# Last down product of the second block: low parts of the weights on VectorE, its and TensorE's order pinned unit by unit, normalised rows in tiles of their own

## The chip, the cores and the metric

The kernel runs on one core of one Trainium2 chip. Its time is the device time of one execution in microseconds; for the kernel before, three executions took 2285.23, 2288.1 and 2289.94 us, so the median is 2288.1 us. Lower is better.

## What is computed

A trunk of two layers over 1024 rows of 1024 numbers in float32. Each layer has a token mixer (latent attention in the first, differential attention in the second) and a SwiGLU block, both with a residual and a layer norm:

```python
def _swiglu(x, w_gu, w_down):
    gate, up = jnp.split(x @ w_gu, 2, axis=-1)
    return (jax.nn.silu(gate) * up) @ w_down
...
    h = _layernorm(ALPHA * h + _swiglu(h, ffn_w_gu[i], ffn_w_down[i]), ln_ffn_g[i], ln_ffn_b[i])
```

The change concerns the very last part of this: the end of `@ w_down` of the second layer, and the layer norm of the rows that it completes, which are stored as the output.

## The kernel before, in words

**Products in three passes.** TensorE multiplies fp32r operands. A float32 operand is split into a high part (a cast on ScalarE, L503) and a low part (the difference, L504, on VectorE or GpSimd); a product of two such pairs is high x high, high x low and low x high, three matmuls (`step`, L815 on).

**The down product in seven.** The down product of a block is cut into halves in each of its three dimensions and done as seven products of half-size blocks (Strassen's scheme), so the operands of most of them are sums or differences of blocks. The hidden values come from a DRAM scratch `h_dr`, already combined; the blocks of the weights are combined on the fly. Each product has 11 units (11 slices of 128 along the hidden dimension). A unit needs one tile of hidden values `op_h` (made by `from_h`) and one tile of weights, and gives three matmuls for each of four accumulators, one PSUM bank for each 128 rows (`t` or `tb`, 0 to 3).

**The last product**, named "4", adds to the four banks `dw_0` to `dw_3`, which hold the result of the product before it. For each unit j, the work ahead of the matmuls is

- on VectorE, `rw_t` minus `tt` (L805): the weights of this product are the difference of a block that is loaded in three groups (`rw_t`, in `w_block`) and a block kept from before (`tt`);
- on ScalarE two casts (L503), to the high parts `wt` and `op_h`;
- the two low parts (L504): that of the hidden values on VectorE, that of the weights on GpSimd (`split(..., G)`).

In the last block (`next_x is None`) the loop over the units issues only the banks 0 and 1; then `last(0)` and `last(1)` close them, and the banks 2 and 3 follow, each with all 11 units. `last(t)` adds the bank to its residual row block `z` (L834, the sum comes out too) and normalises it. `layer_norm` (L163 on) gives the means on VectorE (L166, L167), two sums of squares on ScalarE (L170), `y = (z - mean) * g` on VectorE (L176), the variance (L178), its power on GpSimd (L180), and `y * rs + b` on VectorE (L183), which is stored by SyncE's DMA queue. Here y is z itself: the row block is overwritten in place.

**What sets the order.** Every engine executes its own list in order. A scheduler makes the lists by priority and by its own estimate of when things are ready; `behind(i, j)` (L155 on) holds instruction i after instruction j in a list without a wait. Before the change the low parts of `op_h` and the subtractions L805 are held only behind the reads of the banks (`banks_read[-1]`). Loads are issued by SyncE's queue in the order in which `load_down` was called.

Of the kernel before, what the change touches and what calls it, by code (L numbers as in the profile page):

```python
# [9 lines left out]
F32 = mybir.dt.float32  # L10
F32R = mybir.dt.float32r
AF = mybir.ActivationFunctionType
ALU = mybir.AluOpType
# [29 lines left out]
def trunk(  # L43
# [33 lines left out]
    V, A, G, T = nc.vector, nc.scalar, nc.gpsimd, nc.tensor  # L77
# [29 lines left out]
    def f32(t):  # L107
        return t.bitcast(F32)

    def big_tile(name, dt=F32R):  # L110
        return big.tile([P, 2, 1024], dt, tag="big", name=name)
# [43 lines left out]
    def behind(i, j):  # L155

        tc.add_manual_dep(
            i, j.name,
            mybir.DependencyInfo(mybir.DependencyClass.NoSync, mybir.DependencyReason.DATA),
            reason="kept in program order",  # L160
        )
# [186 lines left out]
    class OutProj:  # L348
# [54 lines left out]
        def split(self, tb, hs, o):  # L403
            oh, ol = (t[:, hs] for t in self.oh[tb])
            A.activation(oh, o, AF.Copy, scale=self.scale)
            V.scalar_tensor_tensor(ol, o, self.scale, f32(oh), ALU.mult, ALU.subtract)
# [99 lines left out]
    turns = {"op": 0}  # L506

    def op_unit(src, eng, name, tags=("wh", "wl"), pool=None):

        tag = tags[turns["op"] % len(tags)]  # L510
        turns["op"] += 1
        where = wp if tag in ("wh", "wl") else pool
        t = where.tile([P, 2, 512], F32R, tag=tag, name=f"op_{name}", bufs=6 if pool is where else 3)
        turns["last"] = split((t[:, 0], t[:, 1]), src, eng)
        return t

    def swap(side):
        return "left" if side == "right" else "right"

    def ffn(side, xo, xst, pending, layer, x_src, x_dst, lng, lnb, next_x, spare=()):  # L520
# [4 lines left out]
        nm = f"f{layer}"  # L525
# [10 lines left out]
        r, tmp, ops, acc, hp, pg = {}, {}, {}, {}, {}, {}  # L536
# [192 lines left out]
        for i in (1, 0):  # L729
# [7 lines left out]
        lo_half, hi_half = slice(0, 512), slice(512, 1024)  # L737
# [3 lines left out]
        tt = {  # L741
            j: poolx.tile([P, 2, 512], F32, tag=f"tt{j}", name=f"tt{layer}_{j}")
            for j in (range(11) if swap(side) == "left" else reversed(range(11)))
        }

        chain, in_order, banks_read = [], [], []

        def load_down(dst, src):

            i = nc.sync.dma_start(dst, src).ins  # L750
            if in_order:
                behind(i, chain[-1])
            chain.append(i)

        def from_h(s, name, tags=tags, late=False):

            for gi, (j0, j1) in enumerate(groups):
                r = poolh.tile([P, 4, 512], F32, tag="rawh", name=f"rh{layer}_{name}_{gi}")
                load_down(r[:, :j1 - j0], h_dr[gi][s, :, :j1 - j0, :])
                for j in range(j0, j1):  # L760
                    t = op_unit(r[:, j - j0], V, f"h{layer}_{name}_{j}", tags, pool)
                    if late and j > 1:
                        behind(turns["last"], banks_read[-1])
                    yield t

        def w_block(kh, cs, name):

            for gi, (j0, j1) in enumerate(groups):
                r = big_tile(f"rw{layer}_{name}_{gi}", F32).rearrange("p a (b c) -> p (a b) c", b=2)
                src = w_dn[layer, 11 * kh + j0:11 * kh + j1, :, cs].rearrange("f p c -> p f c")  # L770
                load_down(r[:, :j1 - j0], src)
                for j in range(j0, j1):
                    yield r[:, j - j0]

        def unit(src, name, eng=G, tags=tags):
            return op_unit(src, eng, f"w{layer}_{name}", tags, pool)


        def b11():
            for j in range(11):  # L780
                load_down(tt[j], w_dn[layer, j].rearrange("p (b c) -> p b c", b=2))
                yield unit(tt[j][:, 0], f"b11_{j}", V if j < early else G)
# [18 lines left out]
                yield unit(r, f"{name}_{j}")  # L801

        def t4():
            for j, r in enumerate(w_block(1, lo_half, "t4")):
                i = V.tensor_tensor(r, r, tt[j][:, 0], ALU.subtract).ins  # L805
                if j > 1:
                    behind(i, banks_read[-1])
                if next_x is not None:
                    yield unit(r, f"t4_{j}", G, ("o",))
                    continue  # L810
                t = poolx.tile([P, 2, 512], F32R, tag=f"tt{j}", name=f"wt4{layer}_{j}")
                split((t[:, 0], t[:, 1]), r, G)
                yield t

        def step(o, h, w, tb, first, last):  # L815
            c = slice(tb * P, (tb + 1) * P)
            for a, b_ in ((0, 0), (0, 1), (1, 0)):
                T.matmul(  # L818
                    o, h[:, a, c], w[:, b_], start=(first and (a, b_) == (0, 0)), stop=(last and a == 1),
                    skip_group_check=True,  # L820
                )

        def whole(o, hs, ws, first):
            for j, (h, w) in enumerate(zip(hs, ws)):
# [7 lines left out]
        def added(half, cs, o, tb, acc=None, scale=1.0):  # L832
            n = rows(half, tb)
            banks_read.append(V.scalar_tensor_tensor(  # L834
                z[n][:, cs], z[n][:, cs], scale, o, ALU.mult, ALU.add,
                **({} if acc is None else {"accum_out": sums[n][:, acc:acc + 1]}),
            ).ins)

        def finish(tb, junk, y=None):
            y = z[tb] if y is None else y  # L840
            return layer_norm(z[tb], sums[tb], junk, y, g, b, f"{nm}_{tb}", x_dst[tb * P:(tb + 1) * P, :],
                              2 if next_x is None and tb == 3 else 1)

        def accumulators(name, tag):
            if tag == "x":
                return [ps_s(f"d{name}{layer}_{t}") for t in range(4)]
            return [(ps_m if t < 2 else ps_t)(f"d{name}{layer}_{t}") for t in range(4)]
# [5 lines left out]
        hs, ws = from_h(0, "1"), b11()  # L853
        with tc.high_priority(100):
            hs, ws = (itertools.chain([next(x) for _ in range(early)], x) for x in (hs, ws))
        x4, y4 = accumulators("x", "x"), accumulators("y", "y")
# [6 lines left out]
        hs = from_h(3, "5")  # L863
        hs = itertools.chain([next(hs)], hs)
# [17 lines left out]
        y4 = accumulators("w", "y")  # L882
# [11 lines left out]
        for t in range(4):  # L894
            added(1, hi_half, y4[t], t, 1)

        def last(t):
            added(1, lo_half, y4[t], t, 0)
            finish(t, [y4[t], y4[t]])

        new, rest, normed = None, [], []
        if next_x is None:
            hs, ws = [], []
            for h, w in zip(from_h(2, "4", late=True), t4()):
                hs.append(h)
                ws.append(w)
                for t in range(2):
                    step(y4[t], h, w, t, False, len(hs) == 11)
            stx.close()
            last(0)  # L910
            last(1)
            for t in range(2, 4):
                for j in range(11):
                    step(y4[t], hs[j], ws[j], t, False, j == 10)
                last(t)
        else:
            gb = big_tile(f"gb_{nm}", F32)
            for i, src in enumerate((lng, lnb)):
                nc.gpsimd.dma_start(gb[:, i], src.partition_broadcast(P))
            whole(y4, from_h(2, "4", ("o",)), t4(), False)  # L920
            stx.close()
            new = next_x()
            with tc.high_priority(60):
                for t in range(4, 8):
                    to_xT(z[t], new, t, f"{nm}_{t}", (ps_s, ps_s))

            yb = [big_tile(f"y_{nm}_{i}", F32) for i in range(2)]
            junk = wp.tile([P, 2, 512], F32, tag="wr", name=f"junk_{nm}", bufs=2)
            for t in range(4):
                y = yb[t // 2][:, t % 2]  # L930
                V.scalar_tensor_tensor(
                    y[:, lo_half], z[t][:, lo_half], 1.0, y4[t], ALU.mult, ALU.add, accum_out=sums[t][:, 0:1]
                )
                A.copy(y[:, hi_half], z[t][:, hi_half])
            for t in range(4):
                y = yb[t // 2][:, t % 2]
                normed.append(layer_norm(
                    y, sums[t], [junk[:, 0], junk[:, 1]], y, gb[:, 0], gb[:, 1], f"{nm}_{t}",
                    x_dst[t * P:(t + 1) * P, :],
                ))  # L940
                rest.append(lambda t=t, y=y: to_xT(y, new, t, f"{nm}_{t}", (ps_t, ps_s)))
# [24 lines left out]
    with tc.tile_pool(name="a0", bufs=2, side="right") as pool:  # L966
# [92 lines left out]
        done = []  # L1059
        for tbs in ((0, 1), (2,), (3,), (4,), (5,), (6,), (7,)):  # L1060
# [6 lines left out]
            done = [(tb, latents(tb, *m)) for tb, m in zip(tbs, ms)]  # L1067
# [179 lines left out]
    with ExitStack() as st:  # L1247
# [11 lines left out]
        for ql in q_lo:  # L1259
            for mp in range(2):  # L1260
                b = slice(64 - mp * 64, 128 - mp * 64)
                z = bb[b, :512]
                i = G.tensor_tensor(ql[b, mp * 512:mp * 512 + 512], z, z, ALU.subtract).ins
# [260 lines left out]
```

## Time and profile before

| what | value |
|---|---|
| median of three executions | 2288.1 us (2285.23 to 2289.94) |
| the profiled execution's own time | 2289.88 us |
| its span, first to last instruction | 2288.1 us |
| TensorE busy, share of the span | 2245.8 us, 98% |
| VectorE, ScalarE, GpSimd busy | 1556.8, 1015.4, 864.0 us |
| granted TensorE clock, mean | 0.997 |

All times in the profile are microseconds from the start of the span, so the profiled execution spends 1.78 us outside of it. The last product's matmuls stand from 2242.45 on. A row of the timeline gives start, duration, engine, line, operation, output and inputs, and in brackets how long the engine was idle ahead of it and what ended that. Consecutive instructions of an engine overlap by a little: the step from one start to the next is what each costs in a row.

### The profile page before, as it was taken

Reading aid. Unit: us, or ns where it says so; the run is one execution under the profiler, and the core shown is the slowest. Engines: PE = TensorE matmul, PEld = TensorE weight load, DVE = VectorE, ACT = ScalarE, POOL = GpSimd, SP = SyncE. Lnnn points to the kernel's source line nnn. Section 1 sums busy time; section 2 is a strip of 40 time slices with the busy share of each in tenths; the row PEclk is TensorE's granted clock in tenths of the full one; section 3 lists DMA queues with packets and bytes.
Section 4 is the critical chain, followed back from the end, with each engine's and each line's share of the span. In section 5 each row is a group of like instructions: output and inputs, shape, how many; then the busy total and the mean of one; then the engine's idle time right before and its main releaser. Section 6 shows DMA issues by size and latency. Waiting matters only on the chain.

```text
span 2288.1 us, 31118 instructions
## 1 busy us (share of the span) xinstructions
PE 2245.8 (98%) x11410; PEld 1913.3 (84%) x11410; DVE 1556.8 (68%) x2837; ACT 1015.4 (44%) x2097; POOL 864.0 (38%) x687
## 2 busy tenths in 40 slices
PE   8999999999999999999999999999999999999997
PEld 8999998878888887888889898988778888877886
DVE  5676665686666658677576666676776665668777
ACT  4455564342333324344465655564432333234353
POOL 2232341114444435555432423221024444436563
PEclk9999999999999999999999999999999999999998
DMA  5010125334444428444311212154254131338353
GB/s 201 14 35 31 41 72 198 140 132 151 151 152 179 151 103 331 184 179 149 106 45 31 70 28 66 33 200 155 92 175 143 69 138 69 138 115 317 132 205 119
DMA packets 105544, 288.28 MB, mean 126 GB/s; under 512 B 7968, under 2 KB 30112, under 8 KB 94896
## 3 DMA queue, kind: packets, MB, share of 16 engines
q1 hardware_dynamic: 100976, 275.87, 33.9%
q0 software_dynamic: 4416, 10.42, 1.6%
q8 instruction: 90, 1.47, 0.3%
q14 instruction: 62, 0.51, 0.1%
HBM read 205.00 MB, written 77.07 MB: 123 GB/s over the span
## 4 chain that ended last, share of the span: by engine, by line
PE 90%; DVE 4%; DMA 3%; issue 1%; ACT 1%; POOL 1%; SPq 0%; DVEq 0%; POOLq 0%; ACTq 0%
PE gb L549 14%; PE gc L549 10%; PE ga L549 10%; PE dw L818 7%; PE s_a L219 4%; PE zp_a L417 3%; PE dx L818 3%; PE s_b L219 3%; PE dv L818 3%; PE dy L818 3%; PE bp L145 3%; PE bp L143 3%; PE bp L144 3%; PE o_a L262 2%; PE o_b L262 2%; PE hq L1023 1%
## 5 line engine op out<-in xcount | busy, mean ns | idle before, releaser
L503 ACT CAST op_g<-gr 128x512 fp32r<-128x512 f32 x240 | 146.8, 621 | 370.1 <-PE gb L549 182.3
L504 POOL TENSOR_TENSOR op_g<-gr,op_g 128x512 fp32r<-128x512 f32 x104 | 146.6, 1415 | 247.9 <-ACT op_g L503 139.9
L504 DVE TENSOR_TENSOR op_h<-rh,op_h 128x512 fp32r<-128x512 f32 x154 | 162.5, 1083 | 63.7 <-ACT op_h L503 63.6
L549 PE MATMUL ga<-xh_m,op_g 128*128 128x512 f32 x512 | 168.2, 389 | 0.0
L503 ACT CAST op_h<-rh 128x512 fp32r<-128x512 f32 x154 | 92.9, 620 | 139.7 <-PE dx L818 38.0
L818 PE MATMUL dw<-op_w_t,op_h 128*128 128x512 f32 x660 | 151.3, 390 | 0.0
L818 PEld LDWEIGHTS dw<-op_w_t,op_h 128*128 128x128 f32 x660 | 123.5, 188 | 26.0 <-DVE op_h L504 0.4
L227 ACT ACTIVATE l_b<-l_b,mx_b 128x256 f32<-128x256 f32 (+7 forms) x128 | 99.4, 777 | 76.4 <-DVE mx_b L222 72.4
L818 PE MATMUL dx<-op_w_b,op_h 128*128 128x512 f32 x528 | 122.5, 391 | 7.4 <-ACT op_w_b L503 3.9
L1328 POOL TENSOR_SCALAR l_b<-l_b,rb,cst 128x128 f32<-128x128 f32 (+3 forms) x64 | 52.5, 820 | 204.4 <-DVE rb L1327 193.0
L504 POOL TENSOR_TENSOR op_w_t<-tt,op_w_t 128x512 fp32r<-128x512 f32 x66 | 98.7, 1499 | 80.7 <-ACT op_w_t L503 80.1
L818 PEld LDWEIGHTS dx<-op_w_b,op_h 128*128 128x128 f32 x528 | 98.5, 188 | 31.0 <-ACT op_w_b L503 4.7
L504 DVE TENSOR_TENSOR op_g<-gr,op_g 128x512 fp32r<-128x512 f32 x136 | 110.6, 819 | 14.5 <-ACT op_g L503 14.3
L549 PE MATMUL gb<-t4h_f,op_g 128*128 128x512 f32 x352 | 115.9, 390 | 3.7 <-DVE tmp L632 3.7
L504 POOL TENSOR_TENSOR op_g<-s,op_g 128x512 fp32r<-128x512 f32 x40 | 54.8, 1369 | 170.1 <-ACT op_g L503 161.9
L549 PE MATMUL gb<-t2h_f,op_g 128*128 128x512 f32 x352 | 115.6, 390 | 0.4 <-DVE op_g L504 0.4
L549 PE MATMUL gc<-t1h_f,op_g 128*128 128x512 f32 x352 | 115.6, 389 | 0.1
L549 PE MATMUL gc<-b22h_f,op_g 128*128 128x512 f32 x352 | 115.3, 389 | 0.0
L549 PE MATMUL gb<-t3h_f,op_g 128*128 128x512 f32 x352 | 115.2, 389 | 0.0
L549 PEld LDWEIGHTS ga<-xh_m,op_g 128*128 128x128 f32 x512 | 96.1, 188 | 20.0
L143 PE MATMUL bp<-xT_f,h_wb 128*128 128x512 f32 x256 | 101.7, 397 | 0.0
L144 PE MATMUL bp<-xT_f,h_wb 128*128 128x512 f32 x256 | 101.5, 397 | 0.0
(382 smaller groups left out, 6736.7 us busy)
## 6 DMA issues: line engine op xcount, KB each, us to landing
gr<-in_w_gu SPq DMA_DIRECT2D x44, 1024.0 KB, 6.9
rh<-h_dr SPq DMA_DIRECT2D x28, 1024.0 KB, 5.1
h_dr<-sh SPq DMA_DIRECT2D x22, 1024.0 KB, 5.0
h_dr<-hp SPq DMA_DIRECT2D x22, 768.0 KB, 4.1
tt<-in_w_dn SPq DMA_DIRECT2D x22, 512.0 KB, 8.0
rh<-h_dr SPq DMA_DIRECT2D x14, 768.0 KB, 4.4
wo_dr<-op_pwo SPq DMA_DIRECT2D x16, 512.0 KB, 3.5
z<-xs_dr SPq DMA_DIRECT2D x16, 512.0 KB, 10.2
```

The source lines that it names most:

```text
L143: T.matmul(ps_out, lh, rh, start=(i == 0), stop=False)
L144: T.matmul(ps_out, lh, rl, start=False, stop=False)
L145: T.matmul(ps_out, ll, rh, start=False, stop=(i == n - 1))
L219: T.matmul(s[:, :w], lh, rh[:, ks], start=(j == 0), stop=(j == len(q_pass) - 1))
L227: ends["exp"] = A.activation(l[:, :n], l[:, :n], AF.Exp, bias=mx, scale=-1.0, accum_out=sm).ins
L262: T.matmul(po[:, c], a, b[:, j % 2, c], start=st, stop=sp_, skip_group_check=True)
L417: T.matmul(m, a[:, h, :], self.wo[h][w][:, c], start=(start and h == heads[0] and a is oh and w == 0), stop=(stop and h == heads[-1] and a ...
L503: A.copy(hi, src)
L504: return eng.tensor_tensor(lo, src, f32(hi), ALU.subtract).ins
L549: T.matmul(o, w[:, a, kc], x[b][:, k, :], start=(first and k == 0 and (a, b) == (0, 0)), stop=(k == 3 and a == 1), skip_group_check=True,)
L818: T.matmul(o, h[:, a, c], w[:, b_], start=(first and (a, b_) == (0, 0)), stop=(last and a == 1), skip_group_check=True,)
L1328: G.tensor_scalar(l1[:, :n], l1[:, :n], r[:, 1:2], nlam, ALU.mult, ALU.mult)
```

## The change

Four things, all in the last block's last product:

- `t4` makes the low parts of the weights on VectorE (V in place of G).
- Their order is written out: the subtraction of unit j + 1 ahead of the weights' low part of unit j, the next unit's subtraction behind the last conversion of hidden values (`turns["last"]`), and that conversion behind the last low part of weights (`w_low`). The subtractions are produced two units ahead, so the load of a group of weights is called, and issued, before that of the hidden values of the same group.
- On TensorE the units of bank 2 are held behind the units of banks 0 and 1 three further on, and those of bank 3 behind all 33 before (`done`).
- Each row block is normalised into a tile of its own (`ys`, two tiles of the ring of large buffers for four row blocks) in place of z.

```diff
--- before.py
+++ after.py
@@ -743,7 +743,7 @@
             for j in (range(11) if swap(side) == "left" else reversed(range(11)))
         }
 
-        chain, in_order, banks_read = [], [], []
+        chain, in_order, banks_read, w_low = [], [], [], []
 
         def load_down(dst, src):
 
@@ -760,7 +760,7 @@
                 for j in range(j0, j1):
                     t = op_unit(r[:, j - j0], V, f"h{layer}_{name}_{j}", tags, pool)
                     if late and j > 1:
-                        behind(turns["last"], banks_read[-1])
+                        behind(turns["last"], (banks_read + w_low[2:])[-1])
                     yield t
 
         def w_block(kh, cs, name):
@@ -801,24 +801,37 @@
                 yield unit(r, f"{name}_{j}")
 
         def t4():
-            for j, r in enumerate(w_block(1, lo_half, "t4")):
-                i = V.tensor_tensor(r, r, tt[j][:, 0], ALU.subtract).ins
-                if j > 1:
-                    behind(i, banks_read[-1])
-                if next_x is not None:
+            def subtracted():
+                for j, r in enumerate(w_block(1, lo_half, "t4")):
+                    i = V.tensor_tensor(r, r, tt[j][:, 0], ALU.subtract).ins
+                    if j > 1:
+                        behind(i, banks_read[-1] if j == 2 or next_x is not None else turns["last"])
+                    yield r, i
+
+            if next_x is not None:
+                for j, (r, _) in enumerate(subtracted()):
                     yield unit(r, f"t4_{j}", G, ("o",))
-                    continue
+                return
+            ready = list(itertools.islice(rows := subtracted(), 2))
+            for j in range(11):
+                r = ready[j][0]
                 t = poolx.tile([P, 2, 512], F32R, tag=f"tt{j}", name=f"wt4{layer}_{j}")
-                split((t[:, 0], t[:, 1]), r, G)
+                if j:
+                    ready += itertools.islice(rows, 1)
+                i = split((t[:, 0], t[:, 1]), r, V)
+                if 1 < j < 10:
+                    behind(i, ready[j + 1][1])
+                w_low.append(i)
                 yield t
 
         def step(o, h, w, tb, first, last):
             c = slice(tb * P, (tb + 1) * P)
-            for a, b_ in ((0, 0), (0, 1), (1, 0)):
+            return [
                 T.matmul(
                     o, h[:, a, c], w[:, b_], start=(first and (a, b_) == (0, 0)), stop=(last and a == 1),
                     skip_group_check=True,
-                )
+                ).ins for a, b_ in ((0, 0), (0, 1), (1, 0))
+            ]
 
         def whole(o, hs, ws, first):
             for j, (h, w) in enumerate(zip(hs, ws)):
@@ -894,25 +907,27 @@
         for t in range(4):
             added(1, hi_half, y4[t], t, 1)
 
-        def last(t):
+        def last(t, y):
             added(1, lo_half, y4[t], t, 0)
-            finish(t, [y4[t], y4[t]])
+            finish(t, [y4[t], y4[t]], y)
 
         new, rest, normed = None, [], []
         if next_x is None:
-            hs, ws = [], []
+            hs, ws, done = [], [], []
             for h, w in zip(from_h(2, "4", late=True), t4()):
                 hs.append(h)
                 ws.append(w)
-                for t in range(2):
-                    step(y4[t], h, w, t, False, len(hs) == 11)
+                done += [step(y4[t], h, w, t, False, len(hs) == 11) for t in range(2)]
             stx.close()
-            last(0)
-            last(1)
+            ys = [t[:, i] for t in (big_tile(f"y_{nm}_{i}", F32) for i in range(2)) for i in range(2)]
+            last(0, ys[0])
+            last(1, ys[1])
             for t in range(2, 4):
                 for j in range(11):
-                    step(y4[t], hs[j], ws[j], t, False, j == 10)
-                last(t)
+                    done.append(step(y4[t], hs[j], ws[j], t, False, j == 10))
+                    if j > 1:
+                        behind(done[-1][0], done[2 * min(j + 3, 10) + 1 if t == 2 else 32][2])
+                last(t, ys[t])
         else:
             gb = big_tile(f"gb_{nm}", F32)
             for i, src in enumerate((lng, lnb)):
```

On VectorE, from the last read of the previous product's banks on. In the names, `op_h_4_2` is the hidden tile of product 4, unit 2, `wt_2` its weights, `rw_t_0` the first loaded group. Before:

```order
L834 SCALAR_TENSOR_TENSOR z_3_19118,fs_3_19370<-z_3_19118,dw_3_19818 128x512
L504 TENSOR_TENSOR op_h_4_2_20563<-rh_4_0_20533,op_h_4_2_20563 128x512
L805 TENSOR_TENSOR rw_t_0_20538<-rw_t_0_20538,tt_2_19106 128x512
L504 TENSOR_TENSOR op_h_4_3_20576<-rh_4_0_20533,op_h_4_3_20576 128x512
L805 TENSOR_TENSOR rw_t_0_20538<-rw_t_0_20538,tt_3_19107 128x512
L504 TENSOR_TENSOR op_h_4_4_20591<-rh_4_1_20589,op_h_4_4_20591 128x512
L805 TENSOR_TENSOR rw_t_1_20594<-rw_t_1_20594,tt_4_19108 128x512
L504 TENSOR_TENSOR op_h_4_5_20606<-rh_4_1_20589,op_h_4_5_20606 128x512
```

And in the changed kernel:

```order
L847 SCALAR_TENSOR_TENSOR z_3_19118,fs_3_19370<-z_3_19118,dw_3_19818 128x512
L806 TENSOR_TENSOR rw_t_0_20538<-rw_t_0_20538,tt_2_19106 128x512
L504 TENSOR_TENSOR op_h_4_2_20564<-rh_4_0_20533,op_h_4_2_20564 128x512
L806 TENSOR_TENSOR rw_t_0_20538<-rw_t_0_20538,tt_3_19107 128x512
L504 TENSOR_TENSOR wt_2_20567<-rw_t_0_20538,wt_2_20567 128x512
L504 TENSOR_TENSOR op_h_4_3_20577<-rh_4_0_20533,op_h_4_3_20577 128x512
L806 TENSOR_TENSOR rw_t_1_20581<-rw_t_1_20581,tt_4_19108 128x512
L504 TENSOR_TENSOR wt_3_20580<-rw_t_0_20538,wt_3_20580 128x512
L504 TENSOR_TENSOR op_h_4_4_20594<-rh_4_1_20592,op_h_4_4_20594 128x512
L806 TENSOR_TENSOR rw_t_1_20581<-rw_t_1_20581,tt_5_19109 128x512
```

Two instructions for a unit have become three, and each unit's are finished before the next one's. At the end of the list before stand three conversions of hidden values in a row (`op_h_4_8`, `op_h_4_9`, `op_h_4_10`) and then the three subtractions of the units 8 to 10; now unit 10's low part of weights is the last. The low parts `wt_0` and `wt_1` have come into VectorE's list as well, ahead of the second multiplication of `z_7`.

On TensorE, from unit 4 to unit 7, before:

```order
L818 MATMUL dw_2_19817<-wt_4_20597,op_h_4_4_20591 128x512 x2
L818 MATMUL dw_2_19817<-wt_5_20610,op_h_4_5_20606 128x512
L818 MATMUL dw_0_19815<-wt_6_20623,op_h_4_6_20619 128x512 x2
L818 MATMUL dw_1_19816<-wt_6_20623,op_h_4_6_20619 128x512 x2
L818 MATMUL dw_0_19815<-wt_7_20636,op_h_4_7_20632 128x512
L818 MATMUL dw_1_19816<-wt_7_20636,op_h_4_7_20632 128x512
L818 MATMUL dw_0_19815<-wt_7_20636,op_h_4_7_20632 128x512 x2
L818 MATMUL dw_1_19816<-wt_7_20636,op_h_4_7_20632 128x512 x2
L818 MATMUL dw_0_19815<-wt_8_20653,op_h_4_8_20647 128x512
L818 MATMUL dw_1_19816<-wt_8_20653,op_h_4_8_20647 128x512
L818 MATMUL dw_2_19817<-wt_5_20610,op_h_4_5_20606 128x512
L818 MATMUL dw_0_19815<-wt_8_20653,op_h_4_8_20647 128x512 x2
```

And in the changed kernel:

```order
L830 MATMUL dw_0_19815<-wt_5_20610,op_h_4_5_20607 128x512 x2
L830 MATMUL dw_1_19816<-wt_5_20610,op_h_4_5_20607 128x512 x2
L830 MATMUL dw_2_19817<-wt_2_20567,op_h_4_2_20564 128x512 x3
L830 MATMUL dw_0_19815<-wt_6_20623,op_h_4_6_20620 128x512
L830 MATMUL dw_1_19816<-wt_6_20623,op_h_4_6_20620 128x512
L830 MATMUL dw_0_19815<-wt_6_20623,op_h_4_6_20620 128x512 x2
L830 MATMUL dw_1_19816<-wt_6_20623,op_h_4_6_20620 128x512 x2
L830 MATMUL dw_2_19817<-wt_3_20580,op_h_4_3_20577 128x512 x3
L830 MATMUL dw_0_19815<-wt_7_20636,op_h_4_7_20633 128x512
L830 MATMUL dw_1_19816<-wt_7_20636,op_h_4_7_20633 128x512
L830 MATMUL dw_0_19815<-wt_7_20636,op_h_4_7_20633 128x512 x2
L830 MATMUL dw_1_19816<-wt_7_20636,op_h_4_7_20633 128x512 x2
```

Before, pieces of bank 2 stood as the scheduler had put them, and unit 2 with one matmul of unit 3 of bank 3 came early as well; now unit 2 of bank 2 comes after unit 5 of the banks 0 and 1, then one unit of bank 2 after each further unit, and bank 3 (from unit 2 on) after everything else.

On VectorE, in the normalisation at the end, from the second row block's variance on (`z_1` to `z_3` and `y_f` are row blocks, `y_f_0` holds those of the banks 0 and 1, `y_f_1` the other two). Before:

```order
L178 TENSOR_SCALAR ve_f_1_20712<-ssq_f_1_20708 128x1
L166 TENSOR_SCALAR nmu_f_2_20752<-fs_2_19368 128x1
L167 TENSOR_SCALAR nmu_f_2_20752<-fs_2_19368 128x1
L183 SCALAR_TENSOR_TENSOR z_1_19116<-z_1_19116,rs_f_1_20714,fb_19348 128x1024
L834 SCALAR_TENSOR_TENSOR z_3_19118,fs_3_19370<-z_3_19118,dw_3_19818 128x512
L176 SCALAR_TENSOR_TENSOR z_2_19117<-z_2_19117,nmu_f_2_20752,fg_19346 128x1024
L178 TENSOR_SCALAR ve_f_2_20759<-ssq_f_2_20755 128x1
L166 TENSOR_SCALAR nmu_f_3_20799<-fs_3_19370 128x1
L167 TENSOR_SCALAR nmu_f_3_20799<-fs_3_19370 128x1
L183 SCALAR_TENSOR_TENSOR z_2_19117<-z_2_19117,rs_f_2_20761,fb_19348 128x1024
```

And in the changed kernel:

```order
L178 TENSOR_SCALAR ve_f_1_20714<-ssq_f_1_20710 128x1
L166 TENSOR_SCALAR nmu_f_2_20754<-fs_2_19368 128x1
L167 TENSOR_SCALAR nmu_f_2_20754<-fs_2_19368 128x1
L176 SCALAR_TENSOR_TENSOR y_f_1_20691<-z_2_19117,nmu_f_2_20754,fg_19346 128x1024
L183 SCALAR_TENSOR_TENSOR y_f_0_20690<-y_f_0_20690,rs_f_1_20716,fb_19348 128x1024
L178 TENSOR_SCALAR ve_f_2_20761<-ssq_f_2_20757 128x1
L847 SCALAR_TENSOR_TENSOR z_3_19118,fs_3_19370<-z_3_19118,dw_3_19818 128x512
L183 SCALAR_TENSOR_TENSOR y_f_1_20691<-y_f_1_20691,rs_f_2_20763,fb_19348 128x1024
L166 TENSOR_SCALAR nmu_f_3_20801<-fs_3_19370 128x1
L167 TENSOR_SCALAR nmu_f_3_20801<-fs_3_19370 128x1
L176 SCALAR_TENSOR_TENSOR y_f_1_20691<-z_3_19118,nmu_f_3_20801,fg_19346 128x1024
```

The first multiplication of row block 2 (L176) stands now ahead of the second one of row block 1 (L183) and ahead of the read of `dw_3`, and the second one of row block 2 ahead of the means of row block 3. After these rows only the variance and the second multiplication of row block 3 follow, in both.

## The prediction

> **What bounds the kernel now.** I read the end of the chain of waits first. Its rows give start, duration, and what it consists of:
>
> ```profile
> 2254.97 2.86 DVE op_h L504 x2
> 2257.83 2.53 issue
> 2260.36 1.57 POOL wt L504
> ...
> 2261.98 4.85 PE dw L818 x13
> ...
> 2266.85 1.38 DVE z L834 x4
> ```
>
> In the last product the chain doesn't run on TensorE, but over VectorE's conversions and one of GpSimd, to 2261.98. From there 13 matmuls lead to 2266.83, where bank 0 is complete, and the rest of the chain is VectorE with normalisation. So two things count: when bank 0 is complete, and what VectorE does afterwards.
>
> TensorE's own timeline from the start of the last product:
>
> ```profile
> 2242.45 16.93 PE L818 MATMUL dw<-wt,op_h 128*128 128x512 f32 x74
> 2260.28 0.96 PE L818 MATMUL dw<-wt,op_h 128*128 128x512 f32 x3 [0.90 <-ACT wt L503]
> 2261.98 14.36 PE L818 MATMUL dw<-wt,op_h 128*128 128x512 f32 x55 [0.73 <-POOL wt L504]
> ...
> L818 PE MATMUL dw<-wt,op_h x132: 388/389/628, 2242.5 to 2275.9; 128*128 128x512 f32 x132
> ```
>
> The last row is from the view of the tile `wt` (min, median and max in ns). 74 matmuls take 16.93 us; less the last one's 0.389 that is 16.54 / 73 = 0.2266 us from one to the next. All 132 without a wait would take 131 x 0.2266 + 0.39 = 30.07 us and end at 2272.52. They end at 2261.98 + 14.36 = 2276.34, so 3.82 us are lost. Idle are 0.90 + 0.73 = 1.63. The 55 matmuls at full pace would take 54 x 0.2266 + 0.39 = 12.63 instead of 14.36, another 1.73. The remaining 0.46 is the draining and filling around the two gaps. Where the 1.73 come from is in the windows of 1 us (length, TensorE busy with its count, granted clock, DMA):
>
> ```profile
> 2261.00:2262.00 1.00, 0.27 (x3) 1.00 0.00 0
> 2262.00:2263.00 1.00, 1.00 (x4) 0.81 0.00 0
> 2263.00:2264.00 1.00, 1.00 (x4) 0.50 0.00 0
> ...
> 2265.00:2266.00 1.00, 1.00 (x4) 0.50 0.00 0
> 2266.00:2267.00 1.00, 1.00 (x6) 0.99 0.00 0
> ```
>
> The granted clock is half of full speed for somewhat less than 4 us just behind the gaps.
>
> **Why VectorE is late.** The timeline, VectorE and GpSimd side by side, at the start of the stage:
>
> ```profile
> 2243.27 0.69 DVE L504 TENSOR_TENSOR op_h<-rh,op_h 128x512 fp32r<-128x512 f32 x1
> 2243.87 0.69 DVE L805 TENSOR_TENSOR rw_t<-rw_t,tt 128x512 f32<-128x512 f32 x1
> ...
> 2244.59 0.62 ACT L503 CAST wt<-rw_t 128x512 fp32r<-128x512 f32 x1 [6.24 <-DVE rw_t L805]
> 2245.08 0.69 DVE L805 TENSOR_TENSOR rw_t<-rw_t,tt 128x512 f32<-128x512 f32 x1
> 2245.19 0.33 SPq L750 DMA_DIRECT2D rh<-h_dr  x1
> 2245.29 3.32 POOL L504 TENSOR_TENSOR wt<-rw_t,wt 128x512 fp32r<-128x512 f32 x2 [6.34 <-ACT wt L503]
> ...
> 2245.68 1.78 DVE L504 TENSOR_TENSOR op_h<-rh,op_h 128x512 fp32r<-128x512 f32 x1
> ```
>
> Until GpSimd starts at 2245.29, VectorE's instructions follow each other every 0.60 us. Those that begin inside a GpSimd conversion take up to 1.78 us. The groups over the stage:
>
> ```profile
> L504 POOL TENSOR_TENSOR wt<-rw_t,wt 128x512 fp32r<-128x512 f32 x11 | 17.9, 1647 | 13.9 <-ACT wt L503 11.4 <-issue 2.5
> L504 DVE TENSOR_TENSOR op_h<-rh,op_h 128x512 fp32r<-128x512 f32 x12 | 14.4, 1220 | 0.0
> ...
> L805 DVE TENSOR_TENSOR rw_t<-rw_t,tt 128x512 f32<-128x512 f32 x11 | 9.4, 880 | 0.0
> ```
>
> **Low parts on VectorE, order pinned.** Removed are GpSimd's 11 conversions; VectorE gets 11 more of the shape of its own L504 rows. For units 2 to 10 it has 9 x 3 = 27 instructions from S = 2243.27. With GpSimd empty I price each at 0.60, 16.2 us in all; the other bound is today's mean, which is the slower rival below. The order is subtraction 2, hidden 2, subtraction 3, low 2, hidden 3, subtraction 4, low 3, and so on, so low part j (j = 2 to 9) is instruction 3(j - 1), counted from 0 (unit 10's is the 26th). ScalarE's cast ends 0.72 + 0.62 = 1.34 after the subtraction's start (2243.87 to 2244.59, then 0.62); the low part stands three instructions later, at 1.8, so it does not wait.
>
> TensorE starts at S - 0.82 and has 24 matmuls of units 0 and 1 (5.44), until S + 4.62; a unit for two banks takes 1.36, a unit of bank 2 0.68. It asks for low part 5 at S + 9.15 (third matmul of the unit), 6 at 11.19, 7 at 13.23, 8 at 15.27, 9 at 17.31, 10 at 19.35. VectorE ends them at 7.9, 9.7, 11.5, 13.3, 15.1 and 16.3: at least 1.2 us spare everywhere.
>
> One load can eat this. The third group of hidden values waits for VectorE's conversion of unit 3. That one now ends at S + 3.1 instead of S + 1.9, so the load is issued at 2246.4 (before: 2245.19). The loads in this stretch:
>
> ```profile
> rh<-h_dr SPq DMA_DIRECT2D x2, 1024.0 KB, 5.4
> rw_t<-in_w_dn SPq DMA_DIRECT2D x2, 1024.0 KB, 8.2
> rh<-h_dr SPq DMA_DIRECT2D x1, 768.0 KB, 4.2
> ...
> DMA to landing us min/median/max: 4.2/4.7/6.0
> ...
> 2221.44 0.64 SPq L750 DMA_DIRECT2D rw_t<-in_w_dn  x1
> ...
> 2235.18 3.37 DVE L504 TENSOR_TENSOR op_h<-rh,op_h 128x512 fp32r<-128x512 f32 x2
> ```
>
> After 4.2 us it is there at S + 7.3; ScalarE, whose list is unchanged, casts units 8 to 10 first (1.6) and then the weights of unit 6, by S + 9.5. Low part 6 then starts at 9.5 rather than 9.0 and all later ones shift by 0.5; the least margin is 1.0. TensorE is hit from a landing of 5.1 us on. I take no wait.
>
> The loads of weights have moved ahead of those of hidden values in SyncE's queue, to where their buffers are long free; they only come earlier. But the second group may hold up the first on the way. Twice 8.2 us, and `rw_t_0` (issued 2221.44) would come at 2237.8 instead of 2229.6; the VectorE instructions from there to low part 1 (six of 0.60, one of 1.20, one of 0.13) would end at 2242.7, L183 of `z_7` at 2243.9 and the read of bank 0, without which TensorE may not go on there, at 2244.6: 2.2 after TensorE's present start. Below 3 us of delay nothing would be noticed, since VectorE takes this group at 2232.7 today. 0 to 2.2; I take 0, as the hidden values and the first group are ahead in the queue. The additional early VectorE work (low parts 0 and 1) replaces GpSimd work that now stretches the two conversions beside it to 3.37 us, so it is hidden by TensorE's previous product.
>
> So TensorE ends at 2272.52. Behind bank 0's last matmul stand 2 (bank 1) + 12 (bank 2) + 27 (bank 3) = 41 others: bank 0 is complete at 2272.52 - 41 x 0.2266 = 2263.23 instead of 2266.83. **Gain 3.60.**
>
> **Own tiles for the rows.** The tail as it is:
>
> ```profile
> 2268.39 0.69 ACT L170 ACTIVATE dw<-z,nmu_f 128x512 f32<-128x512 f32 x1 [6.90 <-DVE nmu_f L166]
> ...
> 2270.09 1.28 DVE L176 SCALAR_TENSOR_TENSOR z<-z,nmu_f,fg 128x1024 f32<-128x1024 f32 x1 [1.61 <-ACT dw L170]
> 2271.29 0.21 DVE L178 TENSOR_SCALAR ve_f<-ssq_f 128x1 f32<-128x1 f32 x1
> 2271.42 0.68 DVE L834 SCALAR_TENSOR_TENSOR z<-z,dw 128x512 f32<-128x512 f32 x1
> ...
> 2276.03 1.28 DVE L183 SCALAR_TENSOR_TENSOR z<-z,rs_f,fb 128x1024 f32<-128x1024 f32 x1 [0.42 <-POOL rs_f L180]
> ...
> 2277.24 0.68 DVE L834 SCALAR_TENSOR_TENSOR z<-z,dw 128x512 f32<-128x512 f32 x1
> ...
> 2282.31 0.21 DVE L178 TENSOR_SCALAR ve_f<-ssq_f 128x1 f32<-128x1 f32 x1
> ...
> 2283.18 1.42 DVE L183 SCALAR_TENSOR_TENSOR z<-z,rs_f,fb 128x512 f32<-128x512 f32 x2 [0.66 <-POOL rs_f L180]
> ```
>
> In place, L176 has to wait until ScalarE has read z for its squares: 1.61 us of an engine that is the bound from here on. With its own tile it starts beside them. I replay the new list with T = bank 0 complete, pieces as in these rows: bank reads 0.68 and 0.62, two means 0.25, L176 and L183 1.20, variance 0.13, squares 1.70 to their release, GpSimd 0.86 from the variance's start to L183's. The reads and means 0: to T + 1.54; L176 0 to 2.74; squares until 3.24, variance 0 to 3.37; read of bank 2 (complete at T + 14 x 0.2266 = 3.17) and means 1 to 4.22; L183 0 to 5.42; L176 1 to 6.62; variance 1 and means 2 to 7.00; L176 2 to 8.20; L183 1 to 9.40; variance 2 to 9.53; read of bank 3 (complete at T + 9.29) to 10.13; L183 2 (GpSimd ready at 10.26) to 11.46; means 3 to 11.71; L176 3 beside the squares, until 13.41; variance 3; last L183 at 14.28. Before it is 2283.18 - 2266.85 = 16.33. **Gain 2.05**; the store behind it stays as it is.
>
> **Sum.** -3.60 - 2.05 = -5.65 us, or 0.25%. The profiled execution took 2289.88 us, its changed counterpart 2284.2. It lies 1.8 above the median of the runs, 2288.1; taken off there, 2282.5, my forecast. Everything that differs stands behind 2221, the rest of the lists is the same.
>
> **Rivals.**
>
> The half clock is not the gaps' doing, or not in the median run. There are only 1.63 us idle before it, and a longer stop elsewhere did not bring it:
>
> ```profile
> 2059.51 1.67 PE L818 MATMUL dx<-op_w_b,op_h 128*128 128x512 f32 x6 [1.95 <-ACT op_w_b L503]
> ...
> 2060.00:2061.00 1.00, 1.00 (x6) 1.00 0.39 152
> ```
>
> Where it comes and goes between executions, or stays, 1.73 of the gain are missing: -3.92, 2284.2. For it speaks this stop of 1.95 us with the full clock behind it, against it that the low rows stand right behind the gaps. [...] Chance 0.26.
>
> A new wait in the pinned order: if the third load of hidden values takes its longest, 6.0 us, low part 6 is 0.9 late, and every later unit with it: -4.7, with a half-clock stretch as now -3.0, so 2283.4 to 2285.1. For it: it is issued 1.2 later and ScalarE casts three tiles for late units first; the first group of weights may be late too (above). Against: 4.2 measured. Chance 0.11.
>
> The tail gives nothing, because the last rows are limited by ScalarE and GpSimd one after the other: -3.60, 2284.5. Against: VectorE waits only 0.42 at a time from 2271.29 on until the last variance, so it, not they, sets the pace. Chance 0.10.
>
> Slower: VectorE's long instructions are not GpSimd's doing but its own pace. Then 18 x 1.22 + 9 x 0.88 = 29.9 us are needed, low part 10 comes at S + 29.9 instead of 19.35, bank 0 is 10.5 later than forecast, and the balance is +10.5 - 5.65 = +4.9: 2293.0. It decides from a step of 0.72 us on (26 x 0.72 + 0.69 = 19.4) and makes the kernel slower from (19.35 + 5.65 - 0.69) / 26 = 0.94 on. Against: the steps of 0.60 while GpSimd is idle. Chance 0.06.
>
> **How the numbers follow.** Forecast 0.47, rivals 0.26, 0.11, 0.10, 0.06. About 0.2% (4.6 us) is what a measurement can tell from no change, and my forecast lies 1.1 beyond this; the three runs differ by 4.7. I give the forecast five sixths of its chance beyond (0.39), the first two rivals a quarter to a third (0.10), the third 0.02: faster 0.51; slower 0.06; the same 0.43. The range goes down by 3 from the forecast for the scatter of the runs, and up to 2288.0 to take in the small rivals with the scatter.
>
> **What would show it.** TensorE without a gap over 0.1 us from 2242.45 to about 2272.5 and a granted clock of 1.00 there; L504 and L805 on VectorE at 0.69 us; bank 0 read at about 2263.2; L176 beside L170; the last L183 about 14.3 us behind this read, span 2282.4. Wrong would be: a wait of TensorE for `wt` or `op_h`, VectorE steps over 0.72 us, half clock in the stage, or a tail over 15 us.

## The result and the profile after

The changed kernel takes 2282.7 us (median of 14 executions, 2280.18 to 2284.74), the kernel before in as many executions beside it 2286.49 us (2285.23 to 2289.94). The ratio is 0.9981 with a 95% interval of 0.9974 to 0.9987: faster by 3.8 us (3.0 to 5.9). The interval lies wholly below 1; the size, 0.19%, is just short of the 0.2% that the prediction took as the least that a measurement can tell.

In the profiled executions the span fell by 7.2 us, from 2288.1 to 2280.9. What happened is clearer in the stage that was changed. From here on **the stage** is the time from the first matmul of the last product to the start of the last L183. It has two parts: up to the read of bank 0, and the **tail** behind it. Before, it is 2242.45 to 2283.18, 40.73 us (24.40 and 16.33).

TensorE's timeline of the last product in the changed kernel, and VectorE's groups for it (busy us, mean ns, then idle time ahead; the units 0 and 1, whose rows lie ahead of the stage, are counted too):

```profile
2240.90 30.08 PE L830 MATMUL dw<-wt,op_h 128*128 128x512 f32 x132
```

```profile
L504 DVE TENSOR_TENSOR wt<-rw_t,wt 128x512 fp32r<-128x512 f32 x11 | 7.5, 686 | 0.4 <-ACT wt L503 0.4
L806 DVE TENSOR_TENSOR rw_t<-rw_t,tt 128x512 f32<-128x512 f32 x11 | 7.5, 685 | 0.0
L504 DVE TENSOR_TENSOR op_h<-rh,op_h 128x512 fp32r<-128x512 f32 x11 | 7.4, 684 | 0.0
```

All 132 matmuls run as one piece of 30.08 us, where before there were three with two gaps, and the granted clock is 1.00 to its end. VectorE does eleven instructions more. It spends 22.4 us on these 33, where the 23 in the rows of before (12 and 11, one conversion more than the product has units) took 23.8: with GpSimd out of the way each takes 0.69 instead of 1.22 and 0.88.

The one wait of VectorE among these units is the one for which the prediction had kept a margin. SyncE, ScalarE and VectorE around the third load of hidden values, from the timeline:

```profile
2244.87 0.33 SPq L750 DMA_DIRECT2D rh<-h_dr  x1
...
2249.03 1.66 ACT L503 CAST op_h<-rh 128x512 fp32r<-128x512 f32 x3 [1.16 <-DMA rh<-h_dr]
...
2251.24 0.69 DVE L504 TENSOR_TENSOR wt<-rw_t,wt 128x512 fp32r<-128x512 f32 x1 [0.42 <-ACT wt L503]
```

The load lands some 4.1 us after its issue, ScalarE's three casts for late units come first, and VectorE waits 0.42 us for the weights of unit 6. TensorE notices nothing: its piece of 132 matmuls has no gap.

The tail on VectorE (row blocks 0 to 3, in order of time):

```profile
2261.72 0.69 DVE L847 SCALAR_TENSOR_TENSOR z<-z,dw 128x512 f32<-128x512 f32 x1 [3.16 <-PE dw L830]
...
2263.31 1.28 DVE L176 SCALAR_TENSOR_TENSOR y_f<-z,nmu_f,fg 128x1024 f32<-128x1024 f32 x1
2264.89 0.21 DVE L178 TENSOR_SCALAR ve_f<-ssq_f 128x1 f32<-128x1 f32 x1 [0.29 <-ACT dw L170]
...
2271.26 0.68 DVE L847 SCALAR_TENSOR_TENSOR z<-z,dw 128x512 f32<-128x512 f32 x1
2271.86 0.08 DVE L847 DVE_READ_ACCUMULATOR z<-z,dw 128x1 f32 x1
2272.01 1.28 DVE L183 SCALAR_TENSOR_TENSOR y_f<-y_f,rs_f,fb 128x1024 f32<-128x1024 f32 x1
...
2276.02 1.42 DVE L183 SCALAR_TENSOR_TENSOR y_f<-y_f,rs_f,fb 128x512 f32<-128x512 f32 x2 [0.66 <-POOL rs_f L180]
```

Bank 0 is read 20.82 us after the first matmul, instead of 24.40. The wait of 1.61 us ahead of the first L176 is gone; 0.29 are left ahead of the variance. From the read to the last L183 pass 14.30 us instead of 16.33. The stage is 35.12 us, **5.61 less than in the first profile of before**. The other 1.6 us by which the spans differ lie ahead of the stage: its first matmul is at 2240.90 instead of 2242.45. That is no gain of the change as far as these runs show, since the five profiles of before that there are in all have this matmul anywhere from 2240.55 to 2242.45.

So the stage did in this profile what was forecast, 5.61 for 5.65, and the timed kernels still differ by 3.8. The experiments are about the missing part first, and then about what each part of the change is worth.

### The profile page after: what moved, and what is told of

It is laid out like the page before. It is cut to its first block, busy times and chain, and to the rows that moved or that the text cites. A ratio compares the mean times of both kernels' runs of the same rounds, so it can differ in the third digit from the quotient of the medians.

```text
span 2280.9 us, 31110 instructions
## 1 busy us (share of the span) xinstructions
PE 2242.7 (98%) x11410; PEld 1912.7 (84%) x11410; DVE 1555.2 (68%) x2848; ACT 1015.4 (45%) x2097; POOL 847.9 (37%) x676
## 4 chain that ended last, share of the span: by engine, by line
PE 92%; DVE 3%; DMA 2%; issue 1%; ACT 1%; POOL 0%; SPq 0%; DVEq 0%; POOLq 0%; ACTq 0%
PE gb L549 15%; PE gc L549 10%; PE ga L549 10%; PE dw L830 7%; PE dx L830 5%; PE s_a L219 4%; PE zp_a L417 3%; PE s_b L219 3%; PE dv L830 3%; PE dy L830 3%; PE bp L145 3%; PE bp L143 3%; PE bp L144 3%; PE o_a L262 2%; PE o_b L262 2%; PE hq L1038 1%
## 5 line engine op out<-in xcount | busy, mean ns | idle before, releaser
L504 DVE TENSOR_TENSOR op_g<-gr,op_g 128x512 fp32r<-128x512 f32 x136 | 110.7, 820 | 14.3 <-ACT op_g L503 14.0
```

The costliest lines, as they stand in the source:

```text
L504: return eng.tensor_tensor(lo, src, f32(hi), ALU.subtract).ins
```

## The experiments

**Theory 1**: the two gaps of TensorE in the kernel before are in every execution, but the half clock behind them (a granted clock of 0.50) is only in some; the median execution doesn't have it. **Theory 2**: the half clock always follows these gaps, and the missing 1.8 us were lost elsewhere. Four kernels ran on one chip beside 33 executions of before (median 2287.05 us): before itself, rows in place, the tiles alone, and the low parts with no order pinned. Four ran on another (2286.69): the changed kernel, the two with one set of pins each, and the one with more on the tail. Three single executions of before ran on a third.

### The kernel before, again

No edit.

> The kernel before, unchanged, to see what changes from one execution to the next. The stage is measured from the first matmul of the last product to the start of the last L183: 40.7 us in the first profile of before. Theory 1 (the two gaps of TensorE are always there, the half clock behind them only in some executions): gaps of 0.9 and 0.7 us again, and the stage is either 40.7 us (half clock for almost 4 us) or 38.9 us (full clock). Theory 2 (the half clock always follows these gaps): 40.7 us with half clock. Ratio 1.000 +- 0.0007 in both.

2287.64 us, ratio 1.0004 (0.9995 to 1.0013). The gaps are there again with 0.90 and 0.72 us, but the granted clock is 1.00 to the end of the matmuls, and the stage is 39.24 us. Three more executions of before followed:

> The kernel before, one more look at an execution. Theory 1: the same gaps of 0.9 and 0.7 us, and the stage either 40.7 us with the half clock or 39.2 us without it, both kinds among these three looks and the two profiles there are. Theory 2: 40.7 us each time.

> A second look at the kernel before. Theory 1: gaps as ever, stage 40.7 us with the half clock or 39.2 us without. Theory 2: 40.7 us.

> A third look at the kernel before. Theory 1: gaps as ever, stage 40.7 us with the half clock or 39.2 us without. Theory 2: 40.7 us.

The first of the three, TensorE behind the first piece, and its windows of 1 us (length, busy and count, granted clock, DMA):

```profile
2258.94 0.97 PE L818 MATMUL dw<-wt,op_h 128*128 128x512 f32 x3 [0.89 <-ACT wt L503]
2260.64 14.39 PE L818 MATMUL dw<-wt,op_h 128*128 128x512 f32 x55 [0.73 <-POOL wt L504]
```

```profile
2262.00:2263.00 1.00, 1.00 (x4) 0.50 0.00 0
2263.00:2264.00 1.00, 1.00 (x3) 0.50 0.07 16
```

The third, the same:

```profile
2258.64 0.96 PE L818 MATMUL dw<-wt,op_h 128*128 128x512 f32 x3 [0.89 <-ACT wt L503]
2260.32 12.90 PE L818 MATMUL dw<-wt,op_h 128*128 128x512 f32 x55 [0.72 <-POOL wt L504]
```

```profile
2262.00:2263.00 1.00, 1.00 (x6) 1.00 0.07 16
2263.00:2264.00 1.00, 1.00 (x7) 1.00 0.00 0
```

The same gaps to a hundredth; the 55 matmuls take 14.39 us in one and 12.90 in the other. The stage is 40.72 us in the first and 39.24 in the second and third. Of five profiles of before, two have the half clock (40.7) and three don't (39.24); the kernel with only the tiles of their own (below) has the same gaps, and the half clock, so it is three of six. Theory 2 has fallen. The first half of theory 1 is shown: against an execution without the half clock the change gains 39.24 - 35.12 = 4.1 us, against one with it 5.6. That the median execution lacks it is not shown: the timed 3.8 lies nearest to 4.1, but its interval (3.0 to 5.9) holds 5.6 as well, and the means of the 14 executions differ by 4.4. The cost of the half clock is 1.49 us, not the 1.73 that the prediction had put down to it.

### The changed kernel, again

No edit.

> The changed kernel again, beside the next three on the same chip. Theory 1: no gap and no half clock in the stage, which is 35.1 us whatever the rest of the execution does; ratio 0.9982 (4.1 us: 39.2 without half clock in before, less 35.1). Theory 2 would need 0.9975 (5.6 us).

2282.71 us, ratio 0.9980 (0.9971 to 0.9989), stage 35.12 us once more, no gap. The estimate of theory 1 (0.9982) is met closely; the interval holds theory 2's 0.9975 too, and what speaks against theory 2 are the profiles of before.

### Rows in place, the rest of the change kept

```diff
-            ys = [t[:, i] for t in (big_tile(f"y_{nm}_{i}", F32) for i in range(2)) for i in range(2)]
-            last(0, ys[0])
-            last(1, ys[1])
+            last(0, None)
+            last(1, None)
...
-                last(t, ys[t])
+                last(t, None)
```

> The change without the tiles of their own (rows normalised in place). Both theories: no wait of TensorE, bank 0 is read 20.8 us after the first matmul as in the changed kernel, the tail from there to the last L183 16.3 us instead of 14.3, the stage 37.1 us, 2.0 us over the changed kernel. Ratio to before: 0.9992 by theory 1 (the median execution of before has no half clock, gain 1.8 us), 0.9984 by theory 2 (gain 3.6 us).

2285.26 us, ratio 0.9993 (0.9985 to 1.0002). One piece of 132 matmuls, bank 0 read after 20.83 us, tail 16.31, stage 37.14. The wait ahead of the first L176 is back:

```profile
2267.18 1.28 DVE L176 SCALAR_TENSOR_TENSOR z<-z,nmu_f,fg 128x1024 f32<-128x1024 f32 x1 [1.61 <-ACT dw L170]
```

The order and the move to VectorE are worth 39.24 - 37.14 = 2.1 us of the stage without half clock; the ratio agrees with that (1.6 us), and its interval reaches from 3.4 us to just past zero.

### Only the tiles of their own

```diff
-        def last(t):
+        def last(t, y):
             added(1, lo_half, y4[t], t, 0)
-            finish(t, [y4[t], y4[t]])
+            finish(t, [y4[t], y4[t]], y)
```

and `ys` as in the change.

> The kernel before with only the tiles of their own. Both theories: TensorE's gaps as before, bank 0 read 24.4 us after the first matmul with half clock or 22.6 us without, the tail 14.3 us instead of 16.3, ratio to before 0.9991 (2.0 us). A rival for the tail (its gain hangs on bank 0 coming early): a tail of 15.5 us or more.

2285.07 us, ratio 0.9994 (0.9985 to 1.0002). Bank 0 is read after 24.39 us (this profile has the half clock, and its last 55 matmuls take 14.40 us), the tail is 14.51 us, stage 38.90. The gain of the tail, 1.8 us, does not hang on bank 0 coming early: the rival is out. The ratio (1.4 us, from 3.4 to just past zero) agrees, but would not show it alone. Together with the 2.1 above this makes 3.9 of the 4.1 us. TensorE behind the gaps, and the first rows of this tail:

```profile
2258.91 14.40 PE L818 MATMUL dw<-wt,op_h 128*128 128x512 f32 x55 [0.72 <-POOL wt L504]
...
2263.79 0.69 DVE L834 SCALAR_TENSOR_TENSOR z<-z,dw 128x512 f32<-128x512 f32 x1 [6.07 <-PE dw L818]
...
2265.46 1.28 DVE L176 SCALAR_TENSOR_TENSOR y_f<-z,nmu_f,fg 128x1024 f32<-128x1024 f32 x1
```

L176 starts 1.67 us after the read here, 3.24 in the kernel before.

### The low parts on VectorE, with no order pinned

```diff
-                split((t[:, 0], t[:, 1]), r, G)
+                split((t[:, 0], t[:, 1]), r, V)
```

> The kernel before with only the low parts of the weights moved to VectorE, no order pinned, rows in place. In VectorE's list low part 2 stands behind twelve other instructions, so by steps of 0.60 us it starts at 7.2 and ends at 7.9 us after the last bank read, while TensorE asks for it at 5.5: one gap of 2.4 us, then no other. Bank 0 read about 25.0 us after the first matmul (26.7 with half clock), tail 16.3 us, stage 41.3 to 43.0: the move alone gains nothing, ratio 1.0000 to 1.0015. If instead the move is what pays and not the order, no gap and a stage of 37 us.

2290.62 us, ratio 1.0014 (1.0005 to 1.0023): slower than before. TensorE, and VectorE where it comes to the low parts of the units 2 to 5:

```profile
2239.13 6.51 PE L818 MATMUL dw<-wt,op_h 128*128 128x512 f32 x28
2247.91 25.50 PE L818 MATMUL dw<-wt,op_h 128*128 128x512 f32 x104 [2.27 <-DVE wt L504]
```

```profile
2239.94 0.69 DVE L504 TENSOR_TENSOR op_h<-rh,op_h 128x512 fp32r<-128x512 f32 x1
...
2247.17 2.49 DVE L504 TENSOR_TENSOR wt<-rw_t,wt 128x512 fp32r<-128x512 f32 x4
```

The low part of unit 2 starts 7.23 us after the first of the twelve instructions ahead of it (7.2 was expected), and TensorE stands still for 2.27 us, with the half clock behind it in this profile. Bank 0 is read after 26.84 us, stage 43.22. VectorE's instructions are fast here too (0.69 us each; four in a row take 2.49), so the move alone is not the gain; its place in the list is.

### The pins on TensorE, the low parts still on GpSimd

```diff
+                    done.append(step(y4[t], hs[j], ws[j], t, False, j == 10))
+                    if j > 1:
+                        behind(done[-1][0], done[2 * min(j + 3, 10) + 1 if t == 2 else 32][2])
```

on the kernel before (with `step` returning its matmuls).

> The kernel before with only the pins on TensorE; the low parts of the weights stay on GpSimd, VectorE's order is not pinned, rows in place. VectorE's instructions beside GpSimd stay long (group means near 1.2 and 0.9 us). TensorE has nothing put aside to fill with and waits for the weights of the units 8 to 10, 3 us in all: bank 0 is read 24 us after the first matmul (25.7 with half clock), tail 16.3, stage 40.3 to 42.0, ratio 1.0000 to 1.0012. If TensorE's order alone were the gain, 37.1 us and 0.9991.

2287.93 us, ratio 1.0005 (0.9996 to 1.0014). TensorE has four gaps, the last of 0.95 us, 2.0 in all instead of the 3 expected; bank 0 is read after 24.14 us, stage 40.39. The granted clock is 1.00 to the end of the matmuls here, so this is 1.15 us longer than the 39.24 of before at full clock. VectorE is as slow beside GpSimd as before:

```profile
2258.29 14.13 PE L818 MATMUL dw<-wt,op_h 128*128 128x512 f32 x61 [0.95 <-POOL wt L504]
...
L504 POOL TENSOR_TENSOR wt<-rw_t,wt 128x512 fp32r<-128x512 f32 x11 | 17.8, 1643 | 13.9 <-ACT wt L503 11.4 <-issue 2.5
L504 DVE TENSOR_TENSOR op_h<-rh,op_h 128x512 fp32r<-128x512 f32 x11 | 13.7, 1268 | 0.0
```

### VectorE's order pinned, TensorE's left to the scheduler

```diff
-                    if j > 1:
-                        behind(done[-1][0], done[2 * min(j + 3, 10) + 1 if t == 2 else 32][2])
```

> The change without the pins on TensorE (VectorE's order stays pinned, own tiles stay). No wait of TensorE, end of the matmuls 30.1 us after the first, as in the changed kernel. But the scheduler puts matmuls of the banks 2 and 3 early, and only 32 instead of 41 stand behind bank 0's last: bank 0 is read 22.8 us after the first matmul instead of 20.8. The tail is 14.3 us, the stage 37.1 us, 2.0 us over the changed kernel; ratio 0.9991. If what counts is the end of the matmuls and not bank 0, the stage is 35.1 us and the ratio that of the changed kernel.

2284.45 us, ratio 0.9987 (0.9978 to 0.9996).

```profile
2240.50 30.08 PE L830 MATMUL dw<-wt,op_h 128*128 128x512 f32 x132
```

```profile
2263.36 0.69 DVE L847 SCALAR_TENSOR_TENSOR z<-z,dw 128x512 f32<-128x512 f32 x1 [5.25 <-PE dw L830]
...
2270.61 0.69 DVE L847 SCALAR_TENSOR_TENSOR z<-z,dw 128x512 f32<-128x512 f32 x1 [0.52 <-PE dw L830]
```

TensorE has no gap and ends as early as in the changed kernel, but bank 0 is read after 22.86 us instead of 20.82, and the stage is 36.88, 1.8 longer. The tail is 14.02 us, a little less than the 14.3 expected. So what counts in this stage is not the end of the matmuls but when the first bank is handed to VectorE, which in this run stands still from then on for no more than 0.66 us at a time (once, for 0.52, on account of TensorE).

### One thing more on the tail

```diff
+        if held is not None:
+            held(means)
...
+                if after is not None:
+                    behind(s, after)
```

(`layer_norm` of row block 2 hands out its last multiplication, and that of row block 3 issues it behind its means.)

> The changed kernel with one thing more: the second multiplication of row block 2 (L183 there) is held behind the means of row block 3 on VectorE. Replayed with the same pieces, the means come at 10.1 instead of 11.5 us after bank 0's read, the multiplication fills the time of ScalarE's squares, and the last L183 starts at 13.65 instead of 14.28: tail 13.65, stage 34.5, 0.6 us less than the changed kernel, which the ratio can hardly tell (0.9979 beside 0.9982), but the profile can.

2282.61 us, ratio 0.9979 (0.9970 to 0.9988), beside 2282.71 and 0.9980 for the changed kernel: no difference that can be told. In the profile the tail is 13.77 us and the stage 34.59, 0.53 less. From the end of the tail:

```profile
2269.57 0.68 DVE L856 SCALAR_TENSOR_TENSOR z<-z,dw 128x512 f32<-128x512 f32 x1
...
2270.55 1.28 DVE L186 SCALAR_TENSOR_TENSOR y_f<-y_f,rs_f,fb 128x1024 f32<-128x1024 f32 x1
2271.74 1.28 DVE L178 SCALAR_TENSOR_TENSOR y_f<-z,nmu_f,fg 128x1024 f32<-128x1024 f32 x1
...
2273.80 1.41 DVE L186 SCALAR_TENSOR_TENSOR y_f<-y_f,rs_f,fb 128x512 f32<-128x512 f32 x2 [0.66 <-POOL rs_f L182]
```

(L178 and L186 are L176 and L183 here.) The read of bank 3 to the last multiplication takes 4.23 us instead of 4.76.

## Why the prediction was right, and where not

**The time** (2282.5 forecast, 2282.7 measured) is closer than the reasoning deserved. The gain was forecast as 5.65 us from a median of 2288.1, and was 3.8 from one of 2286.49: the forecast gain was 1.85 too large, the median of three executions stood 1.6 above that of fourteen, and it was luck that two errors of like size met.

**TensorE's gaps and the pinned order: right.** VectorE's step of 0.60 us with GpSimd idle, one piece of 30.07 us (30.08), bank 0 after 20.78 us (20.82), a stall of about 0.5 us at unit 6 on VectorE (0.42) without effect: all as worked out. The slower rival, with VectorE slow by itself, is out (0.69 us an instruction). So is the new wait in the pinned order; the other bound that was taken as 0, a late first group of weights, did not show either: the three groups took 8.8 to 12.7 us to land instead of 6.0 to 8.2, but no instruction waited for one.

**The tail: right.** 14.28 forecast, 14.30 measured, and 14.51 where it was the only change.

**The step that failed is the last one of the sum**, "taken off there": the 5.65 us were worked out against an execution with the half clock and taken off the median whole. The half clock is in two of five profiles of before, and against the other three the stage gains only 4.1 us, so the whole 5.65 can't be taken off an execution of which it isn't known whether it has the half clock. Whether the median one lacks it stays open; the timed 3.8 is nearest to 4.1. The prediction had this as its first rival, with -3.92 us and a chance of 0.26; three of six executions with these gaps are without the half clock, which puts it nearer one half. Two things on record spoke for it: the quoted stop of 1.95 us with full clock behind it, and the profiled execution, which with 2289.88 us was slower than two of the three shown. The term's size was off too, 1.73 for 1.49: the 55 matmuls take 12.90 us with full clock, not the 12.63 that the step of 0.2266 gives. The first matmul behind each gap accounts for 0.11 of the 0.27: in the first profile of before it lasts 0.50 us, where the others last 0.39, at a granted clock of 1.00 and ahead of the half clock. Where the rest stands, no run shows.

**What the parts are worth** was not asked in the prediction: VectorE with the order 2.1 us, the tiles 1.8 to 2.0, and of the first neither the move alone (slower by 3.2 us, 1.1 to 5.3) nor TensorE's pins alone (no difference told) is worth anything. The two orders need each other: without TensorE's pins the stage is 36.88 us. The tiles alone would have 37.4 without the half clock (38.90 - 1.49, an estimate), so the low parts on VectorE in their order bring about 0.5 us by themselves, and TensorE's pins on top of them the other 1.8 (36.88 - 35.12).

## What to carry to other kernels

Moving conversions to the engine that is faster at them (0.69 us each on VectorE with GpSimd out of the way, 1.65 on GpSimd) paid here only with their place in its list, and with TensorE's list fitted to it: the same move was slower by 0.14% when the low parts stood behind twelve other instructions, and gained 2.1 us of the stage when each unit was finished before the next and TensorE took the banks 0 and 1 first. Where a chain ends in an engine with a fixed amount of work, ask when its first input is ready, not when the last matmul ends. And before a gain is worked out from one profile, take out of it what that execution had and another need not have, such as a stretch of half clock.

## What was not expected of the hardware

The half clock does not follow from a gap's length alone. Behind the same two gaps of 0.9 and 0.7 us it came in three executions of six. The stop of 1.95 us at 2058 that the prediction quoted with the full clock behind it has the half clock in the second of the single executions:

```profile
2058.84 2.64 PE L818 MATMUL dx<-op_w_b,op_h 128*128 128x512 f32 x7 [1.95 <-ACT op_w_b L503]
```

```profile
2060.00:2061.00 1.00, 1.00 (x4) 0.50 1.05 412
2061.00:2062.00 1.00, 1.00 (x4) 0.50 1.02 268
```

The windows of 1 us cover this stop in seven profiles, five of before and two of the changed kernel: it lasts 1.95 us in each, and in the other six the granted clock behind it stays 1.00. Each stretch of half clock that the windows show ahead of the matmuls' end, twelve in eight profiles, adds up to 3.40 to 3.42 us (twice what its windows lack of a clock of 1.00). What decides whether the half clock follows, no run shows.

How much idle time it takes is not settled either: a single stop of 1.66 us kept a granted clock of 1.00 in the first profile of before (at 1690), where the two gaps with 1.63 together did not.

Also unexpected, and without effect here: of the two loads of hidden values issued from 2220 on, the first (at 2228.97, ahead of the stage) took 7.9 us to land in the changed kernel, where the longest was 6.0 before. A group of weights is issued right behind it in both kernels, so that alone is not the reason; the groups of weights land later too, as said above, and no run shows the cause:

```profile
DMA to landing us min/median/max: 4.1/6.0/7.9
```
